# A two-block transformer on one Trainium2 core: when the next stage's first weights are split, when a feed-forward stage transposes its first activations, and a Newton step of fewer instructions

## The chip, the core and the metric

The kernel runs on one core of one Trainium2 chip. The engines of the core run side by side and wait for each other by semaphores: TensorE (PE: matrix products and transposes; PEld is its weight load), VectorE (DVE), ScalarE (ACT), GpSimd (POOL) and SyncE (SP, which here only issues DMAs). The metric is the device time of one execution in microseconds (us).

## The reference

256 tokens of width 1024 pass through two blocks of two layers each. In the first block each layer is an attention of four kinds of head and a gated feed-forward; a norm closes the block. In the second block each layer is a half-weighted feed-forward, an attention (stick-breaking in the first layer, sliding-window in the second) and another half-weighted feed-forward.

```python
for l in range(DEPTH):                                  # first block
    h = rms_norm(x, attn_norm[l]);  x = x + mixers(h) @ w_o[l]
    h = rms_norm(x, ffn_norm[l])
    x = x + (silu(h @ w_gate[l]) * (h @ w_up[l])) @ w_down[l]
x = rms_norm(x, final_norm)
for i in range(DEPTH):                                  # second block
    x = x + 0.5 * swiglu(rms_norm_2(x, norm_gains[i, 0]), gate_up[i, 0], down[i, 0])
    x = x + attention_i(rms_norm_2(x, norm_gains[i, 1]))
    x = x + 0.5 * swiglu(rms_norm_2(x, norm_gains[i, 2]), gate_up[i, 1], down[i, 1])
```

## The kernel before, in words

The program is ten stages in a row: attention, feed-forward, attention, feed-forward, then feed-forward, stick-breaking, feed-forward, feed-forward, window attention, feed-forward. Six are feed-forward stages (`ffn`). The 256 tokens are two token tiles, 0 and 1, of 128 each. The order in which code emits instructions is the order on each engine's queue; nothing reorders them (`manual_schedule`).

**Weights.** All weights come as units of 128 x 1024 numbers (512 KB; a few are smaller). A unit is loaded by SP into one of 5 `raw` buffers and then *split*: ACT copies it to a rounded high part `wh` (L224), DVE subtracts to get the low part `wl` (L225). A product is three matmuls (L401 to L403): high by high, high by low, low by high. There are 8 pairs `wh`, `wl`. `pump` splits units ahead until LIVE = 6 are live, `free` gives one back and pumps, `unit` splits on demand when a product finds its unit not split. A split also emits further loads on SP.

**A feed-forward stage.** 22 blocks of 128 hidden columns. The first two blocks are the *head*: four units, made for token tile 0 and then for tile 1, with the tokens as rows (`heads`), then silu and product (`sg`, L521 and L522). These head activations must be transposed by PE (`aT`, L538) before they can be used; they are split into `ah`, `al` (L495, L496). For the blocks f = 2 to 21 gate and up products (`g`, `u`, 24 matmuls of 256 columns each) leave activations already transposed, each with its own `sg` (L552, L553), `ah`, `al`. `sg` has two buffers. `steps` advances `rows_steps`, which makes the down products: for each block c, 6 matmuls of 512 columns for token tile 0 and 6 for tile 1, summed in four PSUM banks.

**The end of a stage** (`rows_steps`, in feed-forward and attention alike). The last SKEW blocks are done for tile 0 first, so that tile 0's residual sum (`residual`, L390 or L392, in two halves) and its norm chain can run while PE does tile 1. The chain is: squares on ACT (L315), sum on DVE (`sv`, L317), a power on POOL (L281) as a guess, a Newton step on DVE (L290 to L295), the scaled and gained tile `xn` on DVE (L327), 8 transposes on PE (`tp`, L371), `hh` on ACT and `hl` on DVE (L495, L496). `held` stops `pump` there. Tile 1's chain runs while PE does the next stage's first products for tile 0; its transposes are put between those (`posts`). `norm_pre` also emits a load of gains on SP, which waits for tile 1's `xn`. After the second layer the norm is applied twice at once (`norm_twice`, L351).

In the text n0, n1, ... are the units of the next stage in order of use; n0 to n3 are a feed-forward stage's head units. The down product of block c is called d(c).

Of the kernel before, what the change touches and what calls it, by code (L numbers as in the profile page):

```python
# [15 lines left out]
ALU = mybir.AluOpType  # L16
# [160 lines left out]
def kernel(ctx: ExitStack, tc: tile.TileContext, x_in, wst, gains, rows, pos, rpb, t5, cst_in, out):  # L177
# [15 lines left out]
    raw = {}  # L193
    split = {}
    done = {"load": 0, "split": 0}
    held, lazy = [False], [False]
    RAW_BUFS, W_BUFS, LIVE = 5, 8, 6

    def load():
# [13 lines left out]
    def flush():  # L213
        while late:
            late.pop(0)()
# [14 lines left out]
    def ahead(n, engine=None):  # L230
        while done["split"] <= min(n, len(units) - 1):
            split_piece(done["split"], engine or DVE)
            done["split"] += 1
# [5 lines left out]
            flush()  # L239
        return split[n]  # L240

    def pump(live=None, engine=None, most=9):
        while not held[0] and len(split) < (live or LIVE) and done["split"] < len(units) and most:
            ahead(done["split"], engine)
            most -= 1

    def free(key):
        del split[index[key]]
# [22 lines left out]
    def gbank(name):  # L271
        return pp.tile([128, 512], F32, name=name, tag="g", bufs=4)
# [5 lines left out]
    def rsqrt_guess(v, w, div):  # L278

        h, y = small(8, "rh")[:, :w], small(8, "ry")[:, :w]  # L280
        POOL.tensor_tensor(out=y, in0=v, in1=mhalf[:, :w], op=ALU.pow)  # L281
        DVE.tensor_scalar(out=h, in0=v, scalar1=-0.5, scalar2=None, op0=ALU.mult)
        return y, h, div

    def rsqrt_step(y, h, div, w):

        t, z = small(8, "rt")[:, :w], small(8, "rz")[:, :w]
        f = div ** 0.5
        if w == 1:
            DVE.scalar_tensor_tensor(out=t, in0=y, scalar=h, in1=y, op0=ALU.mult, op1=ALU.mult)  # L290
        else:
            DVE.tensor_tensor(out=t, in0=y, in1=y, op=ALU.mult)
            DVE.tensor_tensor(out=t, in0=t, in1=h, op=ALU.mult)
        DVE.tensor_scalar(out=t, in0=t, scalar1=f, scalar2=1.5 * f, op0=ALU.mult, op1=ALU.add)
        DVE.tensor_tensor(out=z, in0=t, in1=y, op=ALU.mult)  # L295
        return z

    def rsqrt(v, w, div):
# [12 lines left out]
    def x_rstd(i):  # L311
        ss = small(2, "ss")
        for j in range(2):
            jk = wk.tile([128, 512], F32, name="junk", tag="p", bufs=5)
            ACT.activation(out=jk, in_=x[:, i, j * 512:(j + 1) * 512], func=AF.Square, accum_out=ss[:, j:j + 1])  # L315
        v = small(1, "sv")
        DVE.tensor_scalar(out=v, in0=ss[:, 0:1], scalar1=ss[:, 1:2], scalar2=EPS * D, op0=ALU.add, op1=ALU.add)  # L317
        return rsqrt(v, 1, D)

    xns, xgs = {}, {}  # L320
# [58 lines left out]
    def finish(i, nxt):  # L379

        if nxt == 4:
            norm_twice(i)
        elif nxt is not None:
            norm_pre(nxt, i)
# [54 lines left out]
        if i == 1 and 1 in halves:  # L439
            free(key)  # L440

    SKEW = 5

    def rows_steps(keys, acts, scale, nxt):


        banks = [[dbank("o") for _ in range(2)] for _ in range(2)]
        n = len(keys)

        def ready(c):  # L450
            while acts(c) is None:
                yield "wait"

        for c in range(n - SKEW):
            yield from ready(c)
            for i in range(2):
                rows_product(keys[c], *acts(c), banks, i, first=c == 0)
                yield
        for c in range(n - SKEW, n - 1):
            yield from ready(c)  # L460
            rows_product(keys[c], *acts(c), banks, 0, halves=(0, 1) if c < n - 2 else (0,))
            pump(W_BUFS, DVE, 1)
            yield
        held[0] = True
        rows_product(keys[n - SKEW], *acts(n - SKEW), banks, 1)
        yield
        yield from ready(n - 1)
        rows_product(keys[n - 1], *acts(n - 1), banks, 0, last=True, halves=(0,))
        was, lazy[0] = lazy[0], True
        held[0] = False  # L470
        pump(W_BUFS, DVE, 1)
        held[0] = True
        residual(0, 0, banks, scale, nxt)
        flush()
        lazy[0] = was
        rows_product(keys[n - 2], *acts(n - 2), banks, 0, halves=(1,))
        rows_product(keys[n - 1], *acts(n - 1), banks, 0, last=True, halves=(1,))
        yield
        residual(0, 1, banks, scale, nxt)
        finish(0, nxt)  # L480
        for c in range(n - SKEW + 1, n - 2):
            rows_product(keys[c], *acts(c), banks, 1)
        rows_product(keys[n - 2], *acts(n - 2), banks, 1, halves=(0,))
        rows_product(keys[n - 1], *acts(n - 1), banks, 1, last=True, halves=(0,))
        residual(1, 0, banks, scale, nxt)
        if nxt is not None:
            norm_post(0)
        rows_product(keys[n - 2], *acts(n - 2), banks, 1, halves=(1,))
        rows_product(keys[n - 1], *acts(n - 1), banks, 1, last=True, halves=(1,))
        residual(1, 1, banks, scale, nxt)  # L490
        finish(1, nxt)
        held[0] = False

    def hilo(src, hi, lo):
        ACT.activation(out=hi, in_=src, func=AF.Copy)  # L495
# [6 lines left out]
    def drain(gen):  # L502
        for _ in gen:
            pass


    def ffn(tag, scale, nxt):
        if tag == ("ffn", 0):
            load_hank(1)
        acts = {}  # L510
        heads = [gbank("gu") for _ in range(2)]
        for i in range(2):
            for part, c in (("g", 0), ("u", 256)):
                between = posts(T0, T1) if i == 0 and part == "u" else None
                drain(gemm_b([(tag, part, "head", j) for j in range(2)], {i: heads[i][:, c:c + 256]}, 256, 4, (i,), between))
            if i == 0:
                pump()
        sgs = []
        for i in range(2):
            sg = wk.tile([128, 256], F32, name="sg", tag="sg", bufs=2)  # L520
            ACT.activation(out=sg, in_=heads[i][:, 0:256], func=AF.Silu)  # L521
            DVE.tensor_tensor(out=sg, in0=heads[i][:, 256:512], in1=sg, op=ALU.mult)  # L522
            sgs.append(sg)
        order = [(tag, "d", f) for f in range(NF)]
        down = rows_steps(order, lambda c: acts.get(c), scale, nxt)

        def steps(n):
            for _ in range(n):
                next(down, None)

        for f in range(2, NF):
            ps = gbank("gu")
            drain(gemm_a((tag, "g", f), ps[:, 0:256]))
            if f == 2:
                pt = gbank("aT")
                for i in range(2):
                    for g in range(2):
                        PE.transpose(pt[:, g * 256 + i * 128:g * 256 + (i + 1) * 128], sgs[i][:, g * 128:(g + 1) * 128], ident)  # L538
                for g in range(2):
                    acts[g] = act_tiles()  # L540
                    hilo(pt[:, g * 256:(g + 1) * 256], *acts[g])
            if f == 3:
                steps(2)
            if f == 4 and settled:
                settle()
            if f == 6 and tag == ("ffn", 0):
                prepare_rope()
            if f == 12 and tag == ("ffn", 0):
                na_bias(1)
            drain(gemm_a((tag, "u", f), ps[:, 256:512]))  # L550
            sg = wk.tile([128, 256], F32, name="sg", tag="sg", bufs=2)
            ACT.activation(out=sg, in_=ps[:, 0:256], func=AF.Silu)  # L552
            DVE.tensor_tensor(out=sg, in0=ps[:, 256:512], in1=sg, op=ALU.mult)  # L553
            acts[f] = act_tiles()
            hilo(sg, *acts[f])
            if 3 <= f < NF - 1:
                steps(2 if f < NF - 2 else 1)
                acts.pop(f - 4, None)
        drain(down)


# [504 lines left out]
    def window(nxt):  # L1066
# [6 lines left out]
        def squares(ps, heads, then):  # L1073

            n = 2 * heads
            sq = wk.tile([128, 2, heads, 64], F32, name="sq", tag="v", bufs=3)
            h, y = small(8, "rh")[:, 0:n], small(8, "ry")[:, 0:n]
            ACT.activation(out=sq, in_=ps, func=AF.Square)

            def sums():  # L1080
                ss = small(8, "ss8")[:, 0:n]
                DVE.tensor_reduce(out=ss, in_=sq.rearrange("p i h d -> p (i h) d"), axis=mybir.AxisListType.X, op=ALU.add)
                DVE.tensor_scalar(out=h, in0=ss, scalar1=EPS * 64, scalar2=-0.5, op0=ALU.add, op1=ALU.mult)

            def guess():
                ACT.activation(out=y, in_=h, func=AF.Ln, scale=-2.0)
                ACT.activation(out=y, in_=y, func=AF.Exp, scale=-0.5)

            return [sums, guess, lambda: then((y, h, 64))]
# [330 lines left out]
```

## Time and profile before

| | |
|---|---|
| median of 3 runs | 1639.15 us (1637.87 to 1639.99) |
| the profiled execution, its own time | 1642.52 us |
| its span, first to last instruction | 1640.8 us |
| PE busy | 1593.0 us, 97% of the span |
| DVE busy | 970.5 us, 59% |
| ACT busy | 820.6 us, 50% |
| POOL busy | 59.0 us, 4% |
| mean granted TensorE clock | 0.991 |
| matmuls | 11204 |

The table is of one execution. Matmuls are pipelined: one of 256 columns lasts 0.28 us in the records while the next starts well before its end, so PE's busy share counts a stretch without gaps as full. The idle column of a row, in square brackets, is the time in which the engine did nothing before it, and the arrow names what ended it. The granted clock is 1.00 at 2.4 GHz and 0.50 at 1.2 GHz.

### The profile page before, as it was taken

Reading aid. Unit: us, or ns where it says so; the run is one execution under the profiler, and the core shown is the slowest. Engines: PE = TensorE matmul, PEld = TensorE weight load, DVE = VectorE, ACT = ScalarE, POOL = GpSimd, SP = SyncE. Lnnn points to the kernel's source line nnn. Section 1 sums busy time; section 2 is a strip of 40 time slices with the busy share of each in tenths; the row PEclk is TensorE's granted clock in tenths of the full one; section 3 lists DMA queues with packets and bytes.
Section 4 is the critical chain, followed back from the end, with each engine's and each line's share of the span. In section 5 each row is a group of like instructions: output and inputs, shape, how many; then the busy total and the mean of one; then the engine's idle time right before and its main releaser. Section 6 shows DMA issues by size and latency. Waiting matters only on the chain.

```text
span 1640.8 us, 27697 instructions
## 1 busy us (share of the span) xinstructions
PE 1593.0 (97%) x11204; PEld 1459.3 (89%) x11204; DVE 970.5 (59%) x1652; ACT 820.6 (50%) x1405; POOL 59.0 (4%) x86
## 2 busy tenths in 40 slices
PE   7999999999999999999999999999999998999999
PEld 6888999988889998899989989999899988689998
DVE  6786555476765555755555566554755558865553
ACT  5665444357654444544447765443544445754442
POOL 1101000020000000000000000000000002000000
PEclk9999999999999999999999999999999999899999
DMA  8645455444355554465535437555555544345552
GB/s 282 194 127 182 167 194 192 157 163 137 104 168 192 193 193 154 174 206 186 193 124 201 138 104 229 182 192 180 178 194 193 184 163 142 91 136 190 183 187 77
DMA packets 79089, 279.99 MB, mean 171 GB/s; under 512 B 9073, under 2 KB 10609, under 8 KB 78961
## 3 DMA queue, kind: packets, MB, share of 16 engines
q1 hardware_dynamic: 78192, 276.64, 51.0%
q0 software_dynamic: 768, 1.57, 0.5%
q8 instruction: 88, 1.44, 0.4%
q14 instruction: 41, 0.33, 0.1%
HBM read 277.13 MB, written 1.05 MB: 170 GB/s over the span
## 4 chain that ended last, share of the span: by engine, by line
PE 83%; DVE 7%; ACT 4%; DMA 3%; issue 1%; POOL 1%; SPq 0%; ACTq 0%; DVEq 0%; POOLq 0%
PE gu L403 14%; PE gu L401 14%; PE gu L402 14%; PE o L401 8%; PE o L402 8%; PE o L403 8%; DVE wl L225 3%; DMA raw<-in_w_dram 3%; PE s L808 1%; ACT wh L224 1%; PE tp L371 1%; PE k L401 1%; PE k L402 1%; PE k L403 1%; PE q L401 1%
## 5 line engine op out<-in xcount | busy, mean ns | idle before, releaser
L225 DVE TENSOR_TENSOR wl<-raw,wh 128x1024 fp32r<-128x1024 f32 (+2 forms) x510 | 600.5, 1219 | 99.8 <-ACT wh L224 99.1
L401 PE MATMUL gu<-hh,wh 128*128 128x256 f32 x1920 | 541.4, 282 | 0.0
L403 PE MATMUL gu<-hl,wh 128*128 128x256 f32 x1920 | 540.3, 281 | 0.0
L402 PE MATMUL gu<-hh,wl 128*128 128x256 f32 x1920 | 539.9, 281 | 0.0
L224 ACT ACTIVATE wh<-raw 128x1024 fp32r<-128x1024 f32 (+2 forms) x510 | 505.7, 1042 | 36.2 <-DMA raw<-in_w_dram 22.8
L402 PEld LDWEIGHTS gu<-hh,wl 128*128 128x128 f32 x1920 | 362.9, 189 | 4.5
L401 PEld LDWEIGHTS gu<-hh,wh 128*128 128x128 f32 x1920 | 362.6, 189 | 4.5
L403 PEld LDWEIGHTS gu<-hl,wh 128*128 128x128 f32 x1920 | 362.7, 189 | 0.0
L552 ACT ACTIVATE sg<-gu 128x256 f32<-128x256 f32 x120 | 46.1, 384 | 487.6 <-PE gu L403 487.6
L401 PE MATMUL o<-wh,ah 128*128 128x512 f32 x656 | 260.7, 397 | 0.3 <-ACT ah L495 0.3
L402 PE MATMUL o<-wh,al 128*128 128x512 f32 x656 | 258.5, 394 | 0.6 <-DVE al L496 0.6
L403 PE MATMUL o<-wl,ah 128*128 128x512 f32 x656 | 258.5, 394 | 0.0
L553 DVE TENSOR_TENSOR sg<-gu,sg 128x256 f32<-128x256 f32 x120 | 50.9, 424 | 346.4 <-ACT sg L552 346.4
L403 PEld LDWEIGHTS o<-wl,ah 128*128 128x128 f32 x656 | 123.5, 188 | 27.2
L401 PEld LDWEIGHTS o<-wh,ah 128*128 128x128 f32 x656 | 124.1, 189 | 25.3 <-issue 2.8
L402 PEld LDWEIGHTS o<-wh,al 128*128 128x128 f32 x656 | 123.6, 188 | 22.9 <-DVE al L496 0.9
L496 DVE TENSOR_TENSOR al<-sg,ah 128x256 fp32r<-128x256 f32 x120 | 51.0, 425 | 58.0 <-ACT ah L495 58.0
L495 ACT ACTIVATE ah<-sg 128x256 fp32r<-128x256 f32 x120 | 50.1, 418 | 63.7 <-DVE sg L553 63.7
L623 ACT ACTIVATE p<-p,mn 128x256 f32<-128x256 f32 x96 | 46.1, 481 | 31.2 <-DVE mn L620 31.0
L495 ACT ACTIVATE hh<-tp 128x512 fp32r<-128x512 f32 x40 | 23.8, 598 | 71.0 <-PE tp L371 70.4
L403 PE MATMUL gu<-wl,hh 128*128 128x256 f32 x192 | 53.8, 280 | 3.3 <-DVE wl L225 3.3
L401 PE MATMUL gu<-wh,hh 128*128 128x256 f32 x192 | 54.8, 285 | 0.0
(243 smaller groups left out, 1909.5 us busy)
## 6 DMA issues: line engine op xcount, KB each, us to landing
raw<-in_w_dram SPq DMA_DIRECT2D x498, 512.0 KB, 4.4
gb<-in_gains_dram SPq DMA_DIRECT2D x11, 512.0 KB, 4.4
raw<-in_w_dram SPq DMA_DIRECT2D x8, 416.0 KB, 5.2
hank<-in_t_dram SPq DMA_DIRECT2D x8, 192.0 KB, 4.4
hank<-in_rpb_dram POOLq DMA_DIRECT2D x16, 96.0 KB, 4.6
out_dram<-x SPq DMA_DIRECT2D x4, 256.0 KB, 2.0
raw<-in_w_dram SPq DMA_DIRECT2D x2, 384.0 KB, 3.7
x<-in_x_dram SPq DMA_DIRECT2D x2, 256.0 KB, 3.2
```

Source lines behind the costliest of these rows:

```text
L224: ACT.activation(out=hi, in_=src, func=AF.Copy)
L225: late.append(lambda: engine.tensor_tensor(out=lo, in0=src, in1=hi.bitcast(F32), op=ALU.subtract))
L371: PE.transpose(ps[:, k * 128:(k + 1) * 128], xn[:, k * 128:(k + 1) * 128], ident)
L401: PE.matmul(ps, lhsT=lh, rhs=rh, start=first, stop=False)
L402: PE.matmul(ps, lhsT=ll, rhs=rh, start=False, stop=False)
L403: PE.matmul(ps, lhsT=lh, rhs=rl, start=False, stop=last)
L495: ACT.activation(out=hi, in_=src, func=AF.Copy)
L496: DVE.tensor_tensor(out=lo, in0=src, in1=hi.bitcast(F32), op=ALU.subtract)
L552: ACT.activation(out=sg, in_=ps[:, 0:256], func=AF.Silu)
L553: DVE.tensor_tensor(out=sg, in0=ps[:, 256:512], in1=sg, op=ALU.mult)
L623: ACT.activation(out=p[:, sl], in_=p[:, sl], func=AF.Exp, scale=-1.0, bias=mn[:, b:b + 1], accum_out=sm[:, b:b + 1])
L808: PE.matmul(ps[:, i * 256:(i + 1) * 256], lhsT=q[pr, i * 128:(i + 1) * 128], rhs=k[pr, :], start=True, stop=True)
```

## The change

Five edits. (1) `far` lets `pump` go up to 8 live units from block 20 of a feed-forward stage on, and from the start of the last SKEW blocks in any stage, so that n0 to n3 are split before tile 0's residual; no split is emitted between the two halves of that residual any more, and `lazy` and the limits of `pump` are gone. Ahead of the third stage (`nxt == 2`) a fifth unit is split before tile 1's chain. (2) SKEW is 4 instead of 5, and the loop over f emits no step in block 20. (3) A head tile's `sg` follows its own products, the first one ahead of the pump. (4) The `aT` transposes move from block 2 to block 3, and four down steps follow that block's activations where two went before its up product and two behind. (5) The Newton step puts a factor into `h` and fuses its last two instructions; `sv` is made by another instruction.

```diff
-    def pump(live=None, engine=None, most=9):
-        while not held[0] and len(split) < (live or LIVE) and done["split"] < len(units) and most:
-            ahead(done["split"], engine)
-            most -= 1
+    def pump():
+        while not held[0] and len(split) < (W_BUFS if far[0] else LIVE) and done["split"] < len(units):
+            ahead(done["split"])
...
-        DVE.tensor_scalar(out=h, in0=v, scalar1=-0.5, scalar2=None, op0=ALU.mult)
+        DVE.tensor_scalar(out=h, in0=v, scalar1=-0.5 * div ** 0.5, scalar2=None, op0=ALU.mult)
...
-        DVE.tensor_scalar(out=t, in0=t, scalar1=f, scalar2=1.5 * f, op0=ALU.mult, op1=ALU.add)
-        DVE.tensor_tensor(out=z, in0=t, in1=y, op=ALU.mult)
+        DVE.scalar_tensor_tensor(out=z, in0=t, scalar=1.5 * div ** 0.5, in1=y, op0=ALU.add, op1=ALU.mult)
...
-    SKEW = 5
+    SKEW = 4
...
+        far[0] = True
+        pump()
         for c in range(n - SKEW, n - 1):
             yield from ready(c)
             rows_product(keys[c], *acts(c), banks, 0, halves=(0, 1) if c < n - 2 else (0,))
-            pump(W_BUFS, DVE, 1)
             yield
+        yield from ready(n - 1)
         held[0] = True
-        rows_product(keys[n - SKEW], *acts(n - SKEW), banks, 1)
-        yield
-        yield from ready(n - 1)
         rows_product(keys[n - 1], *acts(n - 1), banks, 0, last=True, halves=(0,))
-        was, lazy[0] = lazy[0], True
-        held[0] = False
-        pump(W_BUFS, DVE, 1)
-        held[0] = True
         residual(0, 0, banks, scale, nxt)
-        flush()
-        lazy[0] = was
...
-        for c in range(n - SKEW + 1, n - 2):
+        for c in range(n - SKEW, n - 2):
...
+        if nxt == 2:
+            ahead(done["split"])
         finish(1, nxt)
-        held[0] = False
+        held[0] = far[0] = False
...
-            if f == 2:
+            if f == 3:
                 pt = gbank("aT")
...
-            if f == 3:
-                steps(2)
+            if f == NF - 2:
+                far[0] = True
...
+            held[0] = f == NF - 1
             drain(gemm_a((tag, "u", f), ps[:, 256:512]))
...
             hilo(sg, *acts[f])
-            if 3 <= f < NF - 1:
-                steps(2 if f < NF - 2 else 1)
-                acts.pop(f - 4, None)
+            held[0] = False
+            pump()
+            if 3 <= f < NF - 2:
+                steps(4 if f == 3 else 2)
+            acts.pop(f - 4, None)
```

The window attention's own guess gets the matching factor (-4.0 and -0.25 in place of -0.5 and -2.0).

DVE at the end of the seventh stage and the start of tile 0's chain, before. `x<-o,x` is a half of the residual, `wl` a split, `sg` and `al` belong to block 21, the last rows are the Newton step and the scaled tile.

```order
L553 TENSOR_TENSOR sg<-gu,sg 128x256
L496 TENSOR_TENSOR al<-sg,ah 128x256
L225 TENSOR_TENSOR wl<-raw,wh 128x1024
L392 SCALAR_TENSOR_TENSOR x<-o,x 128x512
L225 TENSOR_TENSOR wl<-raw,wh 128x1024
L392 SCALAR_TENSOR_TENSOR x<-o,x 128x512
L317 TENSOR_SCALAR sv<-ss 128x1
L282 TENSOR_SCALAR rh<-sv 128x1
L290 SCALAR_TENSOR_TENSOR rt<-ry,rh 128x1
L294 TENSOR_SCALAR rt<-rt 128x1
L295 TENSOR_TENSOR rz<-rt,ry 128x1
L327 SCALAR_TENSOR_TENSOR xn<-x,rz,gb 128x512 x2
```

The same place of DVE now:

```order
L544 TENSOR_TENSOR sg<-gu,sg 128x256
L488 TENSOR_TENSOR al<-sg,ah 128x256
L225 TENSOR_TENSOR wl<-raw,wh 128x1024
L389 SCALAR_TENSOR_TENSOR x<-o,x 128x512 x2
L314 SCALAR_TENSOR_TENSOR sv<-ss 128x1
L281 TENSOR_SCALAR rh<-sv 128x1
L288 SCALAR_TENSOR_TENSOR rt<-ry,rh 128x1
L292 SCALAR_TENSOR_TENSOR rz<-rt,ry 128x1
L324 SCALAR_TENSOR_TENSOR xn<-x,rz,gb 128x512 x2
```

The split between the two halves of the residual has gone ahead of `sg`, and the step has one row fewer.

ACT at the start of the eighth stage, from tile 1's norm on, before. `wh` is a split, the first `sg` row the two head tiles, `ah<-aT` the transposed head activations, the last rows block 2.

```order
L224 ACTIVATE wh<-raw 128x1024
L495 ACTIVATE hh<-tp 128x512 x2
L224 ACTIVATE wh<-raw 128x1024 x6
L521 ACTIVATE sg<-gu 128x256 x2
L224 ACTIVATE wh<-raw 128x1024
L495 ACTIVATE ah<-aT 128x256 x2
L224 ACTIVATE wh<-raw 128x1024
L552 ACTIVATE sg<-gu 128x256
L495 ACTIVATE ah<-sg 128x256
```

The same place of ACT now:

```order
L487 ACTIVATE hh<-tp 128x512 x2
L509 ACTIVATE sg<-gu 128x256
L224 ACTIVATE wh<-raw 128x1024 x6
L509 ACTIVATE sg<-gu 128x256
L224 ACTIVATE wh<-raw 128x1024 x2
L543 ACTIVATE sg<-gu 128x256
L487 ACTIVATE ah<-sg 128x256
L224 ACTIVATE wh<-raw 128x1024
L487 ACTIVATE ah<-aT 128x256 x2
L224 ACTIVATE wh<-raw 128x1024
```

The fourth head unit's split has left the first row's place, the head tiles' `sg` stand apart, and `ah<-aT` now comes behind block 2's `sg`, its `ah` and one more split.

## Rows read from the trace of the kernel before

**Rows 1.** PE's waits by releaser: in total, times, the longest (us).
```profile
PE aT L538 <- DVE sg L522: 7.8, 6, 3.1
PE tp L371 <- DVE xn L327: 4.0, 8, 0.9
PE gu L403 <- DVE wl L225: 3.3, 2, 2.0
PE low L403 <- DVE wl L225: 3.2, 2, 1.8
PE tp L371 <- DVE xn L351: 2.4, 1, 2.4
PE v L403 <- DVE wl L225: 1.3, 1, 1.3
PE qkv L403 <- DVE wl L225: 1.3, 1, 1.3
```

**Rows 2.** Timeline of PE, end of the seventh stage: start, duration, instruction, [idle before].
```profile
1152.82 0.39 PE L401 MATMUL o<-wh,ah 128*128 128x512 f32 x1
...
1160.80 0.39 PE L403 MATMUL o<-wl,ah 128*128 128x512 f32 x1
1162.09 1.32 PE L371 MATMUL tp<-cst,xn 128*128 128x128 f32 x8 [0.91 <-DVE xn L327]
...
1164.63 0.28 PE L401 MATMUL gu<-wh,hh 128*128 128x256 f32 x1
...
1168.99 0.28 PE L402 MATMUL gu<-wh,hl 128*128 128x256 f32 x1
1170.56 0.39 PE L403 MATMUL gu<-wl,hh 128*128 128x256 f32 x1 [1.29 <-DVE wl L225]
```

**Rows 3.** Timeline of DVE over the same end of stage.
```profile
1157.10 1.22 DVE L225 TENSOR_TENSOR wl<-raw,wh 128x1024 fp32r<-128x1024 f32 x1
1158.23 0.68 DVE L392 SCALAR_TENSOR_TENSOR x<-o,x 128x512 f32<-128x512 f32 x1
...
1160.65 0.22 DVE L290 SCALAR_TENSOR_TENSOR rt<-ry,rh 128x1 f32<-128x1 f32 x1 [0.54 <-POOL ry L281]
1160.90 0.15 DVE L294 TENSOR_SCALAR rt<-rt 128x1 f32<-128x1 f32 x1
1161.09 0.16 DVE L295 TENSOR_TENSOR rz<-rt,ry 128x1 f32<-128x1 f32 x1
...
1167.95 1.41 DVE L327 SCALAR_TENSOR_TENSOR xn<-x,rz,gb 128x512 f32<-128x512 f32 x2
1169.28 1.22 DVE L225 TENSOR_TENSOR wl<-raw,wh 128x1024 fp32r<-128x1024 f32 x1
```

**Rows 4.** Windows: length, busy time of each engine, PEclk, DMA share, GB/s.
```profile
158.00:166.00 8.00, 6.82 (x36) 6.85 (x37) 4.41 (x8) 3.89 (x8) 0.00 (x0) 0.57 0.70 265
342.00:346.00 4.00, 4.00 (x21) 3.87 (x19) 0.89 (x2) 0.86 (x2) 0.00 (x0) 0.57 0.97 329
656.00:660.00 4.00, 3.48 (x13) 3.15 (x14) 3.71 (x6) 2.04 (x5) 0.00 (x0) 0.57 0.00 0
```

**Rows 5.** Timeline of PE at the head transposes of the last stage.
```profile
1464.86 0.68 PE L538 MATMUL aT<-cst,sg 128*128 128x128 f32 x4 [0.99 <-DVE sg L522]
1465.30 0.36 PE L401 MATMUL gu<-hh,wh 128*128 128x256 f32 x1
```

**Rows 6.** Timeline of ACT: a block's activations and the splits behind them, seventh stage.
```profile
1153.08 0.39 ACT L552 ACTIVATE sg<-gu 128x256 f32<-128x256 f32 x1 [3.89 <-PE gu L403]
1153.96 0.42 ACT L495 ACTIVATE ah<-sg 128x256 fp32r<-128x256 f32 x1 [0.49 <-DVE sg L553]
1154.28 1.99 ACT L224 ACTIVATE wh<-raw 128x1024 fp32r<-128x1024 f32 x2
```

**Rows 7.** Timeline of ACT at the head of the second stage.
```profile
155.83 1.06 ACT L224 ACTIVATE wh<-raw 128x1024 fp32r<-128x1024 f32 x1 [1.70 <-DMA raw<-in_w_dram]
156.90 1.28 ACT L521 ACT_TABLE_LOAD   x1
```

More of the change, by code (lines that the diff above doesn't have):

```diff
@@ L195 @@
     done = {"load": 0, "split": 0}
-    held, lazy = [False], [False]
+    held, lazy, far = [False], [False], [False]
     RAW_BUFS, W_BUFS, LIVE = 5, 8, 6
@@ L287, in rsqrt_step @@
         t, z = small(8, "rt")[:, :w], small(8, "rz")[:, :w]
-        f = div ** 0.5
         if w == 1:
@@ L316, in x_rstd @@
         v = small(1, "sv")
-        DVE.tensor_scalar(out=v, in0=ss[:, 0:1], scalar1=ss[:, 1:2], scalar2=EPS * D, op0=ALU.add, op1=ALU.add)
+        DVE.scalar_tensor_tensor(out=v, in0=ss[:, 0:1], scalar=EPS * D, in1=ss[:, 1:2], op0=ALU.add, op1=ALU.add)
         return rsqrt(v, 1, D)
@@ L510, in ffn @@
         acts = {}
-        heads = [gbank("gu") for _ in range(2)]
+        heads, sgs = [gbank("gu") for _ in range(2)], []
         for i in range(2):
@@ L515, in ffn @@
                 drain(gemm_b([(tag, part, "head", j) for j in range(2)], {i: heads[i][:, c:c + 256]}, 256, 4, (i,), between))
[L516 to L519, printed above, removed]
             sg = wk.tile([128, 256], F32, name="sg", tag="sg", bufs=2)
@@ L523, in ffn @@
             sgs.append(sg)
+            if i == 0:
+                pump()
         order = [(tag, "d", f) for f in range(NF)]
@@ L555, in ffn @@
             hilo(sg, *acts[f])
-            if 3 <= f < NF - 1:
-                steps(2 if f < NF - 2 else 1)
-                acts.pop(f - 4, None)
+            held[0] = False
+            pump()
+            if 3 <= f < NF - 2:
+                steps(4 if f == 3 else 2)
+            acts.pop(f - 4, None)
         drain(down)
@@ L1082, in sums @@
                 DVE.tensor_reduce(out=ss, in_=sq.rearrange("p i h d -> p (i h) d"), axis=mybir.AxisListType.X, op=ALU.add)
-                DVE.tensor_scalar(out=h, in0=ss, scalar1=EPS * 64, scalar2=-0.5, op0=ALU.add, op1=ALU.mult)
+                DVE.tensor_scalar(out=h, in0=ss, scalar1=EPS * 64, scalar2=-4.0, op0=ALU.add, op1=ALU.mult)
             def guess():
-                ACT.activation(out=y, in_=h, func=AF.Ln, scale=-2.0)
+                ACT.activation(out=y, in_=h, func=AF.Ln, scale=-0.25)
                 ACT.activation(out=y, in_=y, func=AF.Exp, scale=-0.5)
```

## The prediction

> **What bounds the kernel now.** I read the waits of PE first, then the timelines of the places that they name, then the granted clock. PE is the engine that sets the end; what can be won is the time in which it waits. At the end of nearly every stage it waits for something that this change touches [rows 1]: for the transposable head activations (`aT`, 7.8 us in six waits, one in each feed-forward stage), for the first `xn` of the next norm (4.0 us in eight waits and 2.4 us in one), and for the `wl` of a unit of the next stage. Of the last kind the change reaches 3.3 + 1.8 + 1.3 + 1.3 = 7.7 us in five waits; the second of the two `low` waits, 3.2 - 1.8 = 1.4 us, belongs to the first stage, which no stage precedes. A wait costs more than its idle time: between the two products around the 1.29 us wait lie 1170.56 - 1168.99 = 1.57 us where (1168.99 - 1164.63) / 37 = 0.118 us is the pace of such products [rows 2], so 1.45 us is lost, 0.16 us beyond the idle time, because the overlap of two products is lost with it.
>
> **The splits.** In the timeline of DVE [rows 3] the reader sees why n3 is late: its `wl` stands behind tile 1's `xn`, at 1169.28, and PE has used up n0 to n2 by then. Now four units are split before tile 0's residual. What would be late next is tile 1's `xn`: its first half is there at 1167.95 + 1.41 / 2 = 1168.66 and PE asks for it after 39 products, at 1164.63 + 39 x 0.118 = 1169.23 [rows 2, 3]. So all 7.7 us go, and 5 x 0.16 = 0.8 us with them. The splits themselves are not more, only earlier: n1's `wh` now stands before block 20's `sg` on ACT and delays it by about 1.0 us [rows 6]; d(20) is used 48 products, 5.7 us, later at the least, which covers it. n2 needs a buffer that block 21's gate product gives back, n3 one that its up product gives back; n3's `wl` follows block 21's `al` on DVE as the first split does now, and is done before PE has finished the first half of tile 0. On SP one weight load more goes ahead of the gains load, which waits for `xn`; that can only bring weights sooner.
>
> **The norm chain of tile 0.** A split of 1.22 us stands between the two halves of the residual, so the second half starts at 1158.23 [rows 3]. PE's 18th product of that stretch ended tile 0: it starts at 1152.82 + 17 x 7.98 / 35 = 1156.70 (the 36 products from 1152.82 to 1160.80 give the pace of 0.228) and lasts 0.39 [rows 2], so the half could have started at about 1157.1: 1.1 us lost. The Newton step loses the 1161.09 - 1160.90 = 0.19 us of L294, and its last instruction turns from L295's form, 0.16, into the fused form, for which L290 shows 0.22 [rows 3]: 0.13 us shorter. In the new order 24 products instead of 18 come before the end of tile 0, but 18 still stand between that and the transposes, so the chain gains 1.26 us on PE. Seven of the eight waits in the first `xn` row and the largest, 0.9 us, are shorter than that; at the ends of attention stages, where the wait is a third of it, less is gained and less needed. I take all 4.0 us, and 1.3 of the 2.4 us (this chain has the norm applied twice and stays exposed): 5.3 us, with 8 x 0.16 = 1.3 us of overlap. If another instruction keeps the half of the residual late, only the step's 0.13 us per wait, 1.2 us, remains; that is the other end.
>
> **The head activations.** The transposes move behind 48 more products, 5.7 us, and the longest of the six waits was 3.1 us [rows 1], so they all go: 7.8 us and 6 x 0.16 = 1.0 us. In exchange something new waits. `sg` has two buffers, both held by the head tiles until `aT`, so block 2's `sg` cannot start before the first two transposes, and block 2's `sg`, `ah`, one split and only then `ah<-aT` stand in ACT's queue. Counted from the start of `aT`: the transposes issue 0.44 us ahead of the next product [rows 5], the first two are done at about 0.4 (estimated from four in 0.68), ACT starts `sg` at 0.45, `ah` 1153.96 - 1153.08 = 0.88 later, the split 1154.28 - 1153.96 = 0.32 after that, at 1.65, and it ends at 2.7 [rows 6]. The split's `wl` on DVE takes from 2.75 to 3.9 (one every 1158.23 - 1157.10 = 1.13 us), and the `al` of the first head block is done at about 4.3. PE needs it for the second product of d(0), at 0.44 + 24 x 0.118 + 0.23 = 3.5. That is a wait of 4.34 - 3.66 = 0.7 us behind the end of the first product, 0.84 with the overlap, in six stages: 5.0 us. Its ends: nothing, if ACT and DVE run a little ahead of this sum, and 0.84 + 1.70 = 2.5 us each, 15.2 us, if the split in that queue has to wait for its weight as long as the split in [rows 7] did.
>
> In four of the six stages a table load for silu now stands ahead of the first `sg`, and n4's split behind that. Load 1.28, `sg` 0.39, `wh` 1.06 and `wl` 1.22 [rows 3, 6, 7] make 3.95 us from the end of tile 1's last `hh`; PE needs n4 after the 48 head products of tile 1, 5.7 us, that start some 0.5 us before. 1.2 us are left, so I cost it at nothing. The Trainium skill (ScalarE: Activation LUTs, section "Table sets: the hidden batching unit") speaks against this: it gives about 2.7 us for a table load. By it the sum would be 5.4 us, n4 would come 0.2 us late, and the four stages would lose an estimated 0.8 us; the row says 1.28 us and decides.
>
> **The clock.** Three windows of 8, 4 and 4 us have a granted clock of 0.57 [rows 4], a mix of full speed and the half level (1.2 GHz). They begin behind the 3.1 us wait for `aT` in the second stage, behind the 1.8 us wait for `wl` in the third and at the 2.4 us wait for `xn` [rows 1], all among those that go or are halved. Lost there: (1 - 0.57) x (6.82 + 4.00 + 3.48) = 6.1 us of PE's busy time. I take all of it; the other end is nothing.
>
> **The sum.** 7.7 + 5.3 + 7.8 = 20.8 us of waits, 3.1 of overlap, 6.1 of clock and some 0.3 for the Newton step in the chains at the start of the kernel: 30.3 us. Against it 5.0 us for d(0), and 0.5 us for small things (in the third stage a fifth split now stands before tile 1's chain; in the window stage two splits now stand before the last head's activations). Net 24.8 us, from 1642.5 us, the profiled execution's own time, to 1617.7. The median of the runs lies 3.4 us below that execution; the forecast for it is 1615 us, rounded.
>
> **Rivals.**
> First, the new wait grows until it eats the gain. Mechanism: the unit split between block 2's `ah` and `ah<-aT` arrives late from memory, ACT stands, and d(0) waits in all six stages. With the 1.70 us of [rows 7] each wait costs 2.5 us, 15.2 in all, and if the clock then falls as in the first window (0.43 x 6.82 = 2.9 us) six times 17.4 more: 32.6 instead of 5.0, 1615 + 27.6 = 1643 us, slower. It decides from a weight that is 1.2 us late, with the clock falling each time (0.84 + 1.2 + 2.9, times six, is 29.8). For it: such lateness stands in the profile. Against: that split is four units later in the stage than the one that waited, and PE comes to it two products' time later.
>
> Second, the clock does not come back: 1621 us. For it: a stretch of half speed begins behind a wait as short as 1.8 us, and six shorter waits come new. Against: all three windows lie right at waits that go. The Trainium skill (TensorE: Matmul & The Clock Gate, section "A second HAM failure mode: psum-queue depth-cycling") says that frequent short gaps between groups of matmuls, not long ones alone, make the clock swing between its two levels; by it these 6.1 us would stay. The six `aT` waits bear it out only in part: 7.8 us in six, of which one stands at a window of [rows 4].
>
> Third, tile 0's residual stays late, because n3's split, right behind block 21, is pushed back by n1 and n2 ahead of it: the chain's 5.3 + 1.3 us shrink to 1.2, 1620 us. For it: DVE has three splits in that stretch. Against: the sum above leaves it room.
>
> Fourth, no wait at d(0): 1610 us. For it: the wait is the difference of two sums of ten terms. Against: every term is a row.
>
> Fifth, the change does not do what it says, because n2 and n3 find no buffer before the stage ends: splits and chain stay, 1615 + 8.5 + 5.4 = 1629 us. Against: the buffers come back with block 21's gate and up products.
>
> **How the numbers follow.** Chances: the forecast 0.46, the first rival 0.06, the second 0.20, the third 0.12, the fourth 0.13, the fifth 0.03. The forecast's own range is 1611 to 1619; the second to fourth rival reach from 1610 to 1621, two of them together to 1626. The range for 8 in 10 is 1606 to 1631: at the lower end no wait at d(0) and the rest of the 2.4 us gone too, at the upper one no clock and d(0) at twice its price and the chain half gained. A measurement of this kernel tells a change from none beyond about 0.2%, 3.3 us. Faster by more than that is every case but the first rival and half of what none of them names: 0.90. Within it 0.04, slower 0.06.
>
> **What would show it.** In the profile after, among PE's waits: no row of `aT` for `sg`, no row of `gu`, `v` or `qkv` for `wl`, `low` with one wait of about 1.4 us, the `xn` of the double norm at about 1.1 us and the other `xn` row gone. A new row of `o` for `al` (six waits of 0.7 us). The three windows at a granted clock of 1.00. Wrong would be: `aT` still waiting; the wait at d(0) above 2 us; or ACT waiting for weights in block 3.

## The result, and the profile after

The changed kernel takes 1612.17 us (median of four executions, 1610.88 to 1613.55) where the kernel before took 1639.57 in the same series: a ratio of 0.9833, 95% interval 0.9816 to 0.9850, so 27.4 us or 1.7% faster. The forecast was 1615 us: 24.8 us less than the profiled execution, brought to the median of the runs. The profiled execution went from 1642.52 to 1613.55 us, its span from 1640.8 to 1611.8: 29.0 us.

The waits of PE after, by releaser, in total, times and the longest (us). They answer to [rows 1]:

```profile
PE tp L368 <- DVE xn L324: 8.2, 1, 8.2
PE o L399 <- DVE al L488: 3.9, 6, 0.6
PE v L398 <- ACT wh L224: 1.3, 1, 1.3
PE low L400 <- DVE wl L225: 0.9, 1, 0.9
PE tp L368 <- DVE xn L348: 0.7, 2, 0.5
```

No `aT` row is left, and no row of `gu`, `v` or `qkv` for `wl`; the one `low` wait and the 8.2 us are the kernel's start. The new row is the one that was forecast: PE waits for `al` in six d(0), 0.64 us each. Without the first wait of the kernel, PE's listed waits (those of 0.2 us and more) add up to 35.9 us before and 19.7 after: 16.2 us less.

The clock did more than the waits let expect. Windows as in [rows 4] (length, busy time of PE, PEld, DVE, ACT, POOL, then PEclk, DMA share, GB/s): the head of the second stage, the start of the third, the double norm, and the window stage after.

```profile
158.00:166.00 8.00, 7.82 (x66) 7.50 (x64) 5.83 (x8) 4.20 (x7) 0.00 (x0) 1.00 0.96 359
340.00:344.00 4.00, 4.00 (x18) 3.93 (x17) 3.01 (x9) 0.60 (x2) 2.30 (x3) 0.58 0.47 138
643.00:647.00 4.00, 3.47 (x21) 2.51 (x20) 3.90 (x8) 2.16 (x5) 0.00 (x0) 1.00 0.00 0
1370.00:1376.00 6.00, 4.93 (x27) 3.48 (x28) 5.75 (x26) 5.37 (x19) 0.00 (x0) 0.72 0.64 175
```

The three windows that the forecast counted are at full speed: rows one and three above show two of them, and the place where `low` waited for `wl` in the third stage has 1.00 as well (334:340). What is low at 340:344 stands behind another wait, of 1.28 us for the `wh` of `v`. The kernel before waits there too (1.17 us at 347.33) and is low behind it, in the first row below, which the forecast did not count. The other two rows are its window stage:

```profile
348.00:352.00 4.00, 3.41 (x15) 3.34 (x16) 3.15 (x13) 1.15 (x2) 1.35 (x2) 0.65 0.45 132
1396.00:1404.00 8.00, 7.43 (x34) 5.04 (x33) 7.06 (x30) 7.26 (x25) 0.00 (x0) 0.57 0.40 131
1426.00:1432.00 6.00, 5.10 (x22) 3.26 (x21) 5.74 (x21) 4.15 (x15) 0.00 (x0) 0.72 0.51 167
```

The mean granted clock of the span rose from 0.991 to 0.998. The two profiled executions lost (1 - 0.991) x 1640.8 = 14.8 and 0.002 x 1611.8 = 3.2 us by it. Over all executions whose clock is listed it is less: 11.1 us in 35 of the kernel before (mean clock 0.9932), 3.0 us in eight of the changed one. So 8.1 of the 28.9 us between their mean times are clock, and 20.8 are waits and what hangs on them.

DVE at the end of the seventh stage, after (start, duration, instruction, [idle before]); it answers to [rows 3]:

```profile
1134.59 1.23 DVE L225 TENSOR_TENSOR wl<-raw,wh 128x1024 fp32r<-128x1024 f32 x1 [0.52 <-ACT wh L224]
1136.38 0.69 DVE L389 SCALAR_TENSOR_TENSOR x<-o,x 128x512 f32<-128x512 f32 x1 [0.57 <-PE o L400]
1137.74 0.69 DVE L389 SCALAR_TENSOR_TENSOR x<-o,x 128x512 f32<-128x512 f32 x1 [0.67 <-PE o L400]
1139.23 0.16 DVE L314 SCALAR_TENSOR_TENSOR sv<-ss 128x1 f32<-128x1 f32 x1 [0.79 <-ACT junk L312]
...
1140.12 0.22 DVE L288 SCALAR_TENSOR_TENSOR rt<-ry,rh 128x1 f32<-128x1 f32 x1 [0.54 <-POOL ry L280]
1140.37 0.16 DVE L292 SCALAR_TENSOR_TENSOR rz<-rt,ry 128x1 f32<-128x1 f32 x1
1140.57 1.42 DVE L324 SCALAR_TENSOR_TENSOR xn<-x,rz,gb 128x512 f32<-128x512 f32 x2
```

Both halves of the residual now wait for PE (0.57 and 0.67 us idle), where before they waited for splits. The step shows 1140.57 - 1140.12 = 0.45 us from `rt` to `xn`, where it took 1161.28 - 1160.65 = 0.63 before ([rows 3] and this row):

```profile
1161.28 1.41 DVE L327 SCALAR_TENSOR_TENSOR xn<-x,rz,gb 128x512 f32<-128x512 f32 x2
```

The chain behind the moved transposes, PE and ACT in the second stage:

```profile
162.15 0.60 PE L528 MATMUL aT<-cst,sg 128*128 128x128 f32 x4
...
162.57 0.38 ACT L543 ACTIVATE sg<-gu 128x256 f32<-128x256 f32 x1 [1.77 <-PE aT L528]
...
163.44 0.42 ACT L487 ACTIVATE ah<-sg 128x256 fp32r<-128x256 f32 x1 [0.49 <-DVE sg L544]
...
163.77 1.05 ACT L224 ACTIVATE wh<-raw 128x1024 fp32r<-128x1024 f32 x1
...
164.72 0.36 ACT L487 ACTIVATE ah<-aT 128x256 fp32r<-128x256 f32 x1
...
165.43 0.39 PE L398 MATMUL o<-wh,ah 128*128 128x512 f32 x1
...
165.99 0.42 DVE L488 TENSOR_TENSOR al<-aT,ah 128x256 fp32r<-128x256 f32 x1
...
166.46 0.50 PE L399 MATMUL o<-wh,al 128*128 128x512 f32 x1 [0.64 <-DVE al L488]
```

Block 2's `sg` waits 1.77 us for a buffer that the transposes give back, then `ah`, a split and only then `ah<-aT`. `al` is done 4.26 us after the transposes began (4.3 in the forecast), and the second product of d(0) starts 1.03 us behind the first where 0.23 is the pace: 0.80 us lost, 0.84 forecast.

### The profile page after: what moved, and what is told of

It reads as the page before. It is cut to its first block, busy times and chain, and to the rows that moved or that the text cites. A ratio compares the mean times of both kernels' runs of the same rounds, so it can differ in the third digit from the quotient of the medians.

```text
span 1611.8 us, 27684 instructions
## 1 busy us (share of the span) xinstructions
PE 1580.2 (98%) x11204; PEld 1452.2 (90%) x11204; DVE 965.8 (60%) x1619; ACT 819.4 (51%) x1405; POOL 59.1 (4%) x86
## 3 DMA queue, kind: packets, MB, share of 16 engines
q8 instruction: 88, 1.44, 0.3%
## 4 chain that ended last, share of the span: by engine, by line
PE 90%; DVE 4%; ACT 2%; DMA 2%; issue 1%; SPq 0%; POOL 0%; DVEq 0%; ACTq 0%; POOLq 0%
PE gu L398 15%; PE gu L399 15%; PE gu L400 15%; PE o L399 9%; PE o L400 9%; PE o L398 9%; DVE wl L225 2%; PE s L801 2%; PE k L398 1%; DMA raw<-in_w_dram 1%; PE k L399 1%; PE k L400 1%; PE q L398 1%; PE v L398 1%; PE v L400 1%; PE q L399 1%
## 5 line engine op out<-in xcount | busy, mean ns | idle before, releaser
L399 PE MATMUL gu<-wh,hl 128*128 128x256 f32 x192 | 54.1, 282 | 0.0
```

Of the source, the lines that this page charges most:

```text
L399: PE.matmul(ps, lhsT=ll, rhs=rh, start=False, stop=False)
```

## The experiments

The ratio is to the kernel before in the same series; the last column is the mean granted clock over the executions.

| run | median us | ratio, 95% interval | clock |
|---|---|---|---|
| the changed kernel again | 1611.64 | 0.9824 (0.9810 to 0.9837) | 0.998 |
| head edits undone | 1617.64 | 0.9855 (0.9841 to 0.9869) | 0.997 |
| splits undone | 1628.43 | 0.9927 (0.9912 to 0.9942) | 0.996 |
| Newton step alone | 1632.82 | 0.9950 (0.9937 to 0.9962) | 0.996 |
| ladder of waits | 1633.24 | 0.9953 (0.9941 to 0.9965) | 0.994 |
| own buffers for head tiles | 1606.32 | 0.9794 (0.9780 to 0.9807) | 0.998 |
| and a sixth unit ahead | 1604.71 | 0.9778 (0.9764 to 0.9791) | 0.998 |
| split between the halves | 1615.08 | 0.9845 (0.9832 to 0.9859) | 0.998 |
| 18 products | 1612.94 | 0.9829 (0.9815 to 0.9842) | 0.998 |
| both of these | 1619.21 | 0.9867 (0.9851 to 0.9882) | 0.998 |
| before, 24 products | 1636.49 | 0.9975 (0.9965 to 0.9986) | 0.994 |

**The parts.** The head edits undone in the changed kernel:

```diff
-            if f == 3:
+            if f == 2:
                 pt = gbank("aT")
...
+            if f == 3:
+                steps(2)
...
-                steps(4 if f == 3 else 2)
+                steps(2)
```

and both head tiles' `sg` behind the second tile's products.

> The changed kernel with edits 3 and 4 undone: both head tiles' silu behind the second head tile's products, the transposes of the head activations in block 2 again. My theory: each edit removes its own waits. Then the six waits for aT come back, 7.8 us with the longest 3.1, the six waits of d(0) (3.9 us) go, and the low clock behind the longest aT wait comes back (2.9 us): 1612.2 + 7.8 - 3.9 + 2.9 = 1619 us, 1616 if the clock stays up. Rival: the aT waits came from head units split too late, so that the early splits alone remove them: no aT wait above 0.2 us, d(0)'s wait gone too, 1608 us.

Measured 1617.64 us. The six `aT` waits came back (7.0 us, the longest 3.0) and d(0)'s went; the clock behind the longest fell for a shorter stretch than before. The rival is out: the early splits alone do not remove an `aT` wait.

The other half: the kernel before with edits 3, 4 and 5.

> The kernel before with edits 3, 4 and 5 alone (head activations and Newton step; the splits and SKEW stay as before). My theory: the wl waits that the splits cause stay (7.7 us in five), the first xn of the norms stays late (6.4 us less 1.2 for the shorter step), the half-speed stretches at the start of the third stage and at the double norm stay; gone are the aT waits and the half-speed stretch behind the longest, 7.8 - 3.9 + 2.9 + 1.5 = 8.3 us: 1631 us. Rival: the two parts depend on each other (a wait that goes in one place lets another start), then the gain of this part and of the other do not add to the 27.4 us of the whole: below 1627 or above 1635.

Measured 1628.43 us, between the theory's 1631 and the bound for "the parts depend on each other". The `wl` waits stayed, the `xn` waits shrank to 2.0 us in three and 2.2 us in one, and six d(0) waits of 0.64 us stand in place of `aT`. Of the missing 2.6 us the Newton step can give the most: the next run shows that it is worth more than was taken for it here.

```diff
-        DVE.tensor_scalar(out=t, in0=t, scalar1=f, scalar2=1.5 * f, op0=ALU.mult, op1=ALU.add)
-        DVE.tensor_tensor(out=z, in0=t, in1=y, op=ALU.mult)
+        DVE.scalar_tensor_tensor(out=z, in0=t, scalar=1.5 * div ** 0.5, in1=y, op0=ALU.add, op1=ALU.mult)
```

> The kernel before with edit 5 alone (the shorter Newton step). My theory: each of the nine waits of tp for xn shrinks by 0.13 us, 6.4 to 5.2 us in all, with some at the kernel's start 1638.1 us. Rival: the step hides behind something else in the chain and the sum stays at 6.4 us, 1639.6 us. A second question to this run: in the window stage the kernel before lost about 5.0 us to a low clock, the changed one 1.5. If that is chance, this kernel, which leaves that stage's order as it was, may show either; if it belongs to the order of work, it shows about 5.

Measured 1632.82 us: 0.5% (0.4 to 0.6), 8.5 us in the medians, far more than either expected. Two things differ. First, each chain became 0.24 us shorter, not 0.13. At the end of the seventh stage (the wait there was 0.91 us, [rows 2]):

```profile
1152.93 0.16 DVE L315 SCALAR_TENSOR_TENSOR sv<-ss 128x1 f32<-128x1 f32 x1 [0.79 <-ACT junk L313]
...
1154.08 0.16 DVE L293 SCALAR_TENSOR_TENSOR rz<-rt,ry 128x1 f32<-128x1 f32 x1
...
1155.08 1.32 PE L369 MATMUL tp<-cst,xn 128*128 128x128 f32 x8 [0.67 <-DVE xn L325]
```

The fused form takes 0.16 us here, not the 0.22 of L290 that the forecast took (L290 reads its scalar from the tile `h`, this one has a constant), and `sv` in its new form 0.16 instead of 0.21. Tile 1's chain, which n3's `wl` waits for, shrank as much: the three waits of 1.29 us went to between 1.04 and 1.08 us. Listed waits of 4.4 us are gone in all. Second, the clock rose from 0.994 (11 executions of the kernel before in this series) to 0.996 (six) in the mean, some 3.4 us. That the shorter step raised it is not shown. In this profile the window stage lost nothing to a low clock (1.00 at 1388:1396 and 1417:1424), with its order as before: what the kernel before lost there is not set by the order alone.

By ratios, with 0.9828 for the changed kernel (the mean of 0.9833 and 0.9824), the step is worth 0.0050, the head edits 0.0023 on top of it (0.0027 as the last part), the splits 0.0099 as the last part (0.0095 before the head edits). They add within what the intervals allow.

**What a wait does to the clock.** In block 10 of each feed-forward stage of the changed kernel:

```diff
+                    for _ in range(k):          # k = 10, 1, 2, 3, 5, 7 by stage
+                        DVE.tensor_copy(out=late_t, in_=ps[:, 0:256])
+                    PE.transpose(gbank("lagp")[:, 0:128], late_t[:, 0:128], ident)
```

> The changed kernel with one wait of a known length put into block 10 of each feed-forward stage: DVE copies the gate product's tile 10, 1, 2, 3, 5 and 7 times (0.42 us each) and PE transposes the copy before it goes on. Idle time added, at 0.2 + 0.42 per copy: 4.4, 0.6, 1.05, 1.5, 2.3 and 3.15 us, 13.0 in all. Theory: a single wait longer than about 2 us sends the clock to half for a stretch that costs 2.9 us, as behind the longest aT wait: three such, 1612.2 + 13.0 + 1.0 + 8.7 = 1635 us, with half-speed windows behind the waits of 4.4, 3.15 and 2.3 us and none behind the others. Rival: a single wait in a busy stretch does not lower the clock, the low windows had another cause: 1626 us and no new low window.

Measured 1633.24 us, nearer to the theory; 21 us slower, of which 13.2 us are the six waits. PE at the three longest, and the window from each on:

```profile
229.49 0.37 PE L539 MATMUL lagp<-cst,lag 128*128 128x128 f32 x1 [4.64 <-DVE lag L538]
...
1239.92 0.45 PE L539 MATMUL lagp<-cst,lag 128*128 128x128 f32 x1 [2.35 <-DVE lag L538]
...
1521.55 0.33 PE L539 MATMUL lagp<-cst,lag 128*128 128x128 f32 x1 [3.27 <-DVE lag L538]
```

```profile
229.00:235.00 6.00, 5.51 (x30) 5.34 (x31) 1.97 (x3) 0.38 (x1) 0.00 (x0) 0.72 0.26 91
1239.00:1245.00 6.00, 5.08 (x28) 4.99 (x29) 1.96 (x3) 0.30 (x1) 0.00 (x0) 0.72 0.49 151
1521.00:1527.00 6.00, 5.45 (x36) 5.05 (x37) 2.44 (x5) 1.71 (x4) 0.00 (x0) 1.00 0.31 94
```

The clock fell behind 4.64 and 2.35 us, and not behind 3.27. The waits of 0.52, 0.97 and 1.44 us show no low window either. Both theories are too simple: a long wait lowers the clock in some cases and not in others. Already in the kernel before a wait of 2.64 us in the window stage (PE, at 1387.84) leaves the window 1384:1396 at 1.00. The same wait for `aT` in the second stage says it again: 3.06 us before, 2.96 with the head edits undone, 3.01 with the Newton step alone, and the windows 158:166 of the last two are (for the first, [rows 4]: 0.57)

```profile
158.00:166.00 8.00, 6.85 (x45) 6.81 (x46) 4.92 (x9) 4.76 (x10) 0.00 (x0) 0.79 0.71 259
```

```profile
158.00:166.00 8.00, 7.06 (x56) 6.90 (x57) 5.19 (x9) 5.51 (x10) 0.00 (x0) 1.00 0.73 259
```

In the mean, the six added waits cost (0.998 - 0.994) x 1630 = 6.5 us of clock.

**The wait at d(0).** The changed kernel as a base, then own buffers:

> The changed kernel once more, as the base for the three runs beside it. 1612 us. If the smaller loss of clock in the window stage belongs to the order of work, the windows there again lose about 1.5 us; if it was chance, up to 5 us.

1611.64 us; the window stage lost about 3 us to the clock here and the third stage nothing, with the same waits in both. So that loss varies between executions too.

```diff
-            sg = wk.tile([128, 256], F32, name="sg", tag="sg", bufs=2)
+            sg = wk.tile([128, 256], F32, name="sg", tag="sgh", bufs=2)
             ACT.activation(out=sg, in_=heads[i][:, 0:256], func=AF.Silu)
```

> The changed kernel with two buffers of their own for the head tiles' sg, so that block 2's sg need not wait for the transposes. My theory (d(0) waits because block 2's sg, its ah and a split stand between the transposes and ah<-aT, and sg has no free buffer): ACT has passed all of that when the transposes come, the six waits of d(0) go: 1612.2 - 3.9 - 6 x 0.16 = 1607.3 us. Rival: not the buffer but the length of the chain behind the transposes sets it, the waits stay at 0.6 us each and the time at 1612 us.

Measured 1606.32 us, 5.3 below its base. No row of `o` for `al` is left. But ACT had not passed everything, as I had expected:

```profile
160.60 0.60 PE L528 MATMUL aT<-cst,sg 128*128 128x128 f32 x4
...
161.28 0.42 ACT L487 ACTIVATE ah<-sg 128x256 fp32r<-128x256 f32 x1 [1.36 <-DVE sg L544]
161.61 1.05 ACT L224 ACTIVATE wh<-raw 128x1024 fp32r<-128x1024 f32 x1
162.56 0.36 ACT L487 ACTIVATE ah<-aT 128x256 fp32r<-128x256 f32 x1
```

The split still stands ahead of `ah<-aT`, which comes 1.96 us behind the start of the transposes instead of 2.57. That 0.6 us is just what d(0) lacked; the margin is thin. So the buffer was the cause, and the size came out right although the way to it was another than expected.

```diff
         finish(1, nxt)
+        if nxt == 2:
+            ahead(done["split"])
         held[0] = far[0] = False
```

> As the run with the head buffers, and ahead of the third stage a sixth unit is split, behind tile 1's norm chain and ahead of its transposes' copies. Theory: the two waits at the start of the third stage (1.28 us for wh, 0.76 behind it) come from that split standing behind both hh of tile 1 on ACT; they go, and with them the half-speed stretch that follows: 1607.3 - 2.0 - 0.3 - 1.7 = 1603.3 us. Rival: the split finds its weight or its buffer late and now holds up hh on ACT, the waits only move: 1607 us or more.

Measured 1604.71 us, the best of all, 2.2% under the kernel before; its interval overlaps that of the own buffers alone. The waits of 1.28 and 0.76 us at the start of the third stage are gone from the trace, the stage took 122.8 us instead of 125.1; the clock gave nothing, since that run's base lost none there. Two d(0) waits of 0.34 and 0.16 us came back, for a reason that I did not follow.

**Why the norm chain was late.** One split back between the halves of tile 0's residual:

```diff
+        was, lazy[0] = lazy[0], True
+        held[0], top[0] = False, 8
+        pump()
+        held[0], top[0] = True, 7
         residual(0, 0, banks, scale, nxt)
+        flush()
+        lazy[0] = was
```

(`top`, 7 at other times, takes the place of `W_BUFS` in `pump`.)

> The changed kernel with one of the early splits of each stage's end put back between the two halves of tile 0's residual; nothing else moves. My theory (that split made the norm chain late by 1.1 us): the nine waits of tp for the first xn come back, less the 0.13 us of the Newton step each, 5.3 us where there are now 0.5, and 8 x 0.16 of overlap: 1612.2 + 4.8 + 1.3 = 1618 us. Rival: the chain was late for another reason (fewer products ahead of the transposes, or the step), the waits stay at 0.5 us and the time at 1612 us.

Measured 1615.08 us: 3.4 above its base, neither 6 nor nothing. Most of the nine waits did not come back: `tp` waits 1.50 us at the double norm, 0.26 at one more end, and under 0.2 at the others. DVE, seventh stage:

```profile
1136.26 0.69 DVE L389 SCALAR_TENSOR_TENSOR x<-o,x 128x512 f32<-128x512 f32 x1 [0.57 <-PE o L400]
1136.87 1.22 DVE L225 TENSOR_TENSOR wl<-raw,wh 128x1024 fp32r<-128x1024 f32 x1
1138.00 0.68 DVE L389 SCALAR_TENSOR_TENSOR x<-o,x 128x512 f32<-128x512 f32 x1
```

The split stands between, yet the second half starts 1.74 us behind the first where PE's pace gives 1137.74 - 1136.38 = 1.36 in the changed kernel: the split costs 0.38 us of spacing, not 1.1. The first half was on time, and PE makes six products between the halves, which hide most of the split. So the other 0.7 us must have another source; in [rows 3] the first half may itself be late, for want of products ahead. Three runs try that; in the changed kernel

```diff
-            if 3 <= f < NF - 2:
-                steps(4 if f == 3 else 2)
+            if 3 <= f < NF - 1:
+                steps(4 if f == 3 else 2 if f < NF - 2 else 1)
```

> The changed kernel with six products of tile 0 (the first step of the last SKEW blocks) put back from behind block 21's activations into block 20, so that 18 products stand before tile 0's end, as in the kernel before, where the change has 24. No split between the halves of the residual, and no other engine's order changes. Theory A (new, after the run with the split between): DVE is late for tile 0's sum only if both hold, 18 products and a split between; with one of them the sum starts at PE's pace. Then nothing happens: no wait of tp above 0.6 us, 1611.6 us. Theory B: the number of products alone made the chain late; then the waits of tp at the ends of feed-forward stages come back, some 0.7 us in three and 2.2 in one: 1615 us.

> Both at once in the changed kernel: 18 products before tile 0's end, and one split between the halves of its residual. Theory A: now the second half is 1.1 us late at the ends of feed-forward stages, and tp waits there as in the kernel before with the short Newton step alone, 0.7 us in three and 2.2 in one, 2.7 us more than with the split between alone: 1615.1 + 3.0 = 1618 us. If the two simply add (theory B): the sum of what each costs alone.

and in the kernel before, with the split of that step kept in its place,

```diff
-            if 3 <= f < NF - 1:
-                steps(2 if f < NF - 2 else 1)
+            if 3 <= f < NF - 2:
+                steps(2)
+            elif f == NF - 2:
+                pump(W_BUFS, DVE, 1)
...
```

> The kernel before with only those six products moved from block 20 behind block 21's activations (24 instead of 18 before tile 0's end); the splits, all other engines' orders and the Newton step stay as before. Theory A: at the five ends of feed-forward stages tp's wait shrinks by 0.84 us (the second half late by 0.26 instead of 1.1): 0.31 and 3 x 0.9 us to about nothing, 2.4 to 1.6; the ends of attention stages and the waits for wl stay: 1640.9 - 3.7 - 0.6 = 1636.6 us. The prediction's theory (the split between the halves is what makes the chain late, however many products come before): no change, 1640.9 us.

Measured 1612.94, 1619.21 and 1636.49 us: near theory A's sums, but not with all of its signs. The times say that the two do not simply add: the split costs 3.4 us with 24 products (1615.08 - 1611.64) and 6.3 with 18 (1619.21 - 1612.94), each pair in one series. PE shows where. From the start of its last product for tile 1 to the first `tp` pass 2.7 us, summed over nine norms, in the changed kernel again; 2.2 more with the split between, 0.7 more with 18 products, 5.3 more with both. At the ends of the fifth, seventh and eighth stage one edit alone costs 0.1 us or nothing, and both cost 0.8. With 18 products the first half is late there too, but the second follows it at once and is on time, as theory A had it (first row below, seventh stage). At the double norm theory A fails: its wait is 0.52 us in the changed kernel, 1.50 with the split, 2.22 with both, so the two add, and 1.23 with 18 products alone, where theory A had no wait above 0.6. There a product with the gains, `xg`, always stands between the halves:

```profile
1135.39 1.32 DVE L389 SCALAR_TENSOR_TENSOR x<-o,x 128x512 f32<-128x512 f32 x2
...
637.01 0.69 DVE L392 TENSOR_TENSOR xg<-x,gb 128x512 f32<-128x512 f32 x1
...
642.21 1.32 PE L368 MATMUL tp<-cst,xn 128*128 128x128 f32 x8 [1.23 <-DVE xn L348]
```

The third run is the kernel before with 24 products and its splits where they were. Its `tp` waits fell from 6.4 to 3.4 us (3.0, where theory A had 3.7), so the prediction's theory is out. That its time met the forecast to 0.1 us is partly luck: its mean clock is 0.994 against 0.993, some 1.6 us of the 3.8, and its longest `aT` wait was 4.6 us instead of 3.1. The kernel with both edits, DVE and PE at the end of the seventh stage:

```profile
1139.61 1.23 DVE L225 TENSOR_TENSOR wl<-raw,wh 128x1024 fp32r<-128x1024 f32 x1 [0.53 <-ACT wh L224]
1140.75 0.68 DVE L389 SCALAR_TENSOR_TENSOR x<-o,x 128x512 f32<-128x512 f32 x1
1141.35 1.22 DVE L225 TENSOR_TENSOR wl<-raw,wh 128x1024 fp32r<-128x1024 f32 x1
1142.48 0.68 DVE L389 SCALAR_TENSOR_TENSOR x<-o,x 128x512 f32<-128x512 f32 x1
...
1146.10 1.32 PE L368 MATMUL tp<-cst,xn 128*128 128x128 f32 x8 [0.69 <-DVE xn L324]
```

and the kernel before with 24 products:

```profile
1151.04 0.69 DVE L392 SCALAR_TENSOR_TENSOR x<-o,x 128x512 f32<-128x512 f32 x1 [0.57 <-PE o L403]
1151.64 1.22 DVE L225 TENSOR_TENSOR wl<-raw,wh 128x1024 fp32r<-128x1024 f32 x1
1152.78 0.68 DVE L392 SCALAR_TENSOR_TENSOR x<-o,x 128x512 f32<-128x512 f32 x1
...
1156.64 1.32 PE L371 MATMUL tp<-cst,xn 128*128 128x128 f32 x8 [0.20 <-DVE xn L327]
```

With 18 products the first half stands right behind the split that follows `al` (no idle time), the second behind the next, and PE waits 0.69 us. With 24 the first half waits for PE (0.57 us), and 0.20 of the 0.91 us of [rows 2] is left, in the kernel before and with its old splits. In that kernel as it was, the first half stood right behind a split, as with both edits:

```profile
1156.50 0.68 DVE L392 SCALAR_TENSOR_TENSOR x<-o,x 128x512 f32<-128x512 f32 x1
```

## Why the prediction was right, and where not

**The splits.** All five `wl` waits that the change can reach are gone, 7.7 us, and what was to be late next, tile 1's `xn`, was not.

**The norm chain of tile 0.** 5.3 us were forecast, 6.4 - 0.7 = 5.7 came, with 0.5 instead of 1.1 us left at the double norm. The size was right and the reason half wrong; that the size came out is luck in part, since the change removed both causes at once. The step that failed is "A split of 1.22 us stands between the two halves of the residual, so the second half starts at 1158.23": of the 1.1 us the split between the halves makes 0.4, and 0.7 come from the first half, which stood behind the split that follows `al` because only 18 products ran beside it. The sentence on 24 instead of 18 products passed over what the six more do. The third rival did not come, nor the fifth: with all five `wl` waits gone, n2 and n3 found their buffers.

**The head activations.** The waits for `aT` went, the new one at d(0) came with the forecast's size and by its mechanism, link by link. ACT waits for no weight between block 2's `ah` and `ah<-aT` in any of the six stages, so the first rival stayed away; nor was there the fourth, no wait. A table load ahead of the first `sg` took 1.28 us in each of four stages after, as in [rows 7], the `sg` starts right behind it (148.43 and 149.72 in the second stage), and no PE wait for n4's `wl` is listed: of the two sums for the head, the row's held.

**The Newton step** is a mis-sized term: 0.24 us a chain instead of 0.13, and tile 1's chains left out. It moved the sum little, since nearly all waits that it shortens were taken whole in the two terms above.

**The clock** is another: 6.1 us forecast, 8.1 in the mean of many executions. The forecast took three low windows for effects of the waits before them. The runs show that such windows come and go with the same waits, and that the window stage's low windows (0.43 x 7.43 + 0.28 x 5.10 = 4.6 us by the rows above) were as open to change. So the size of this term, too, is partly luck. The second rival, that the clock does not come back, is out: the mean rose by 0.005. The Trainium skill (TensorE: Matmul & The Clock Gate, section "A second HAM failure mode: psum-queue depth-cycling") has frequent short gaps swing the clock; the six new waits of 0.64 us did not, around none of them is the clock of the changed kernel low; but they lie 189 to 315 us apart, so no run here shows what frequent ones would do.

The sum: its last step is off by 0.7 us, 1642.5 - 24.8 - 3.4 = 1614.3 and not 1615, and the chances of its named cases add up to 1.00, so that nothing is left for what none of them names. The means lie 28.9 us apart, 4.1 more than the 24.8 forecast. 2.0 of them are clock. The other 2.1 lie in waits and overlap and are not assigned further: the listed waits fell by 16.2 us in the first profile of the changed kernel and by 18.7 in the second, where 20.8 - 4.2 = 16.6 were forecast.

## What to carry to other kernels

Work that stands between a producer and its consumer costs only what the other engine does not cover: before calling a queued instruction the cause of a late chain, count what the bounding engine does in the same stretch, since moving that may cure the chain without touching the queue. A move that removes a wait often makes a new one a few instructions on by a shared buffer; here two small buffers were worth 5.3 us more. Price a low clock behind a wait as an expectation over several executions, not from the one that was profiled.

## What the runs showed of the hardware

The granted clock of one and the same program differs from execution to execution: 0.990 to 0.996 in the kernel before, and a wait of 3.0 us was followed by some 7 us at half speed, by some 3, and by none in three programs. A saving of 0.24 us per norm chain went with a mean clock of 0.996 (six executions) in place of 0.994 (11 in the same series). And the scalar-tensor-tensor form on 128x1 took 0.22 us in `rt`, which reads its scalar from a tile and had waited for POOL just before, and 0.16 us with a constant scalar: in `rz` right behind another DVE instruction and in `sv` behind a wait of 0.79 us for ACT. So a wait alone does not lengthen it; the tile scalar is the likelier reason, but no run changes it alone.
